# A hybrid short-convolution and HGRN2 layer: first-chunk scores of two pairs in one matmul, every second pair of four with its chunks in reverse order, one mask operation, and the second norm's column sums one product later

## The chip, the cores and the metric

The kernel runs on one core of one Trainium2 chip. The metric is the device time of one execution in microseconds (us), the median of several runs. Before the change it is 2642.1 us, from three runs of 2640.95, 2642.10 and 2642.97 us.

## The reference

One layer is applied to 2048 prompt tokens and to 64 tokens of a decoding stream with a state of its own. All arithmetic is in float32, with a model width of 1024. The part that the change touches is the HGRN2 scan: 8 heads of 128 keys and 128 values, in chunks of 64 tokens.

```
h = rms_norm(x, g_pre);  proj = h @ w_in          # ten pieces of 1024 columns
u = cA * vA;  yA = (silu(zA) * bA * causal_conv3(u)) @ w_a_out
fg = lb + (1 - lb) * sigmoid(f);  logf = log(fg);  k = 1 - fg;  q = silu(q) / sqrt(128)
for each chunk of 64 tokens, each head:            # S is the carried state
    b = cumsum(logf);  ref = b[middle]
    att = where(causal, (q * exp(b - ref)) @ (k * exp(ref - b)).T, 0)
    o = att @ v + (q * exp(b)) @ S
    S = exp(b_last) * S + (k * exp(b_last - b)).T @ v
yB = (rms_norm(o) * g_onorm * silu(zB)) @ w_b_out
out = (sigmoid(gA) * yA + sigmoid(gB) * yB) @ w_o
x = x + rms_norm(out, g_post)
x = x + (p @ w_ple_proj) * sigmoid(rms_norm(x, g_ple) @ w_ple_gate)
```

## The kernel before

**Tiling.** The 2112 tokens are worked in three blocks of 704 (`BN`). Tokens lie along the free axis and features on the 128 partitions. Big products are split into high and low parts, three matmuls of 128x352 each for one block of 128 contraction rows, and `sgroup` (lines 358 to 360) runs a seven-product scheme of the Strassen kind: each of the seven products has 4 x 3 = 12 matmuls. `in_turn` (L491 to L493) is the same scheme in another order, and `gemm` (L524 to L526, in `mm3`) is a plain product of 24 matmuls for one half of a block. The weights stream in through DMAs that SyncE issues: `raw` tiles (L194), stored low parts `lo` and `s` (L215); ScalarE casts `raw` to `hi` (L214).

**Hooks.** After each product `hook()` takes one step from a list. So small work, such as a step of attention or of a norm, stands between two products, and the engines run it while TensorE is in the next product. `spread_out` fills that list from tuples of counts: one number for each hook, saying how many steps of a generator it runs. `behind_all` and `placed` fix the order of issue: a step's instructions stand behind the last copies and additions of the products before it, and its matmuls behind the last matmul issued.

**A head.** A block of 704 tokens has 11 chunks: five pairs of two chunks (128 tokens) and one single chunk. They form three parts: four pairs, one pair, and the single chunk. For each of the 24 combinations of block and head, `head_prep` makes the operands on VectorE. `kb` holds the scaled keys of all tokens (L851), `ka` a copy of the first chunk of each pair, packed side by side (L852). In `kb` the first chunk of each pair is then scaled once more by a decay (L853), because queries of the second chunk see it from there. `qe` are the scaled queries, `vt` the values.

**Attention of a part** (`head_attn`), in four steps at four hooks. Step 1 transposes `kb` (L896) and `vt` (L898) by TensorE, 128 columns at a time, into two PSUM banks; ScalarE copies them to `kt` (L900) and `v` (L901). Then, for each pair, one float32 matmul of 64 query columns takes the first-chunk queries against `ka` (L907) and one of 64 columns takes the second-chunk queries against `kb` (L908), into a third bank `p_a` (keys on the partitions, queries along the free axis). Two predicated copies on VectorE move the entries at or below the diagonal into `att`: all columns of the upper 64 partitions (L911), and the second 64 columns of the lower 64 (L912). L911's operand `ka[:, o // 2 : o // 2 + P]` is 128 keys wide, so it holds the first chunk of the next pair too, whose scores the mask drops. The three banks of a step come from a pool of three (`pa`), so that the next part's step 1 needs each bank released. Step 2 (L918) multiplies `kt` by `v`, step 3 (L954, L956) applies `att` and the state, and step 4 (L968) transposes back.

**The norms.** `final_norm` forms the squares of eight row blocks (L633 on ScalarE), adds them up (L634 on VectorE), and then `col_rstd` sums over the partitions by small matmuls with `ones` (L615), one column each. VectorE scales the sums (L586), GpSimd takes the power (L588), and two products later `spread` (L599) brings the result back over the partitions. It does so twice, for `g_post` and for `g_ple`. In each tuple of counts, the second sum's place is one entry:

```
spread_out((norm, (0, 1, 0, 1) + (0, 1, 0) * KB + (1, 0, 1) + (0, 1) * KB))
spread_out((norms[0], (3, 0, 1, 1, 2, 2, 2, 2)), (norms[1], (0, 1, 1, 0, 1, 1, ...)))
```

The first line runs among the gate products of the next block (`sgroup`), after blocks 0 and 1. The second runs in the last block, among the plain products of the gate of block 1.

Of the kernel before, what the change touches and what calls it, by code (L numbers as in the profile page):

```python
# [12 lines left out]
I32 = mybir.dt.int32  # L13
AF = mybir.ActivationFunctionType
ALU = mybir.AluOpType
# [3 lines left out]
P = 128  # L19
D = 1024  # L20
KB = D // P
KH = KB // 2
NH = 8
CH = 64
# [58 lines left out]
def hybrid_step(  # L83
# [17 lines left out]
    V, A, G, T, SP = nc.vector, nc.scalar, nc.gpsimd, nc.tensor, nc.sync  # L101
# [3 lines left out]
    const = ctx.enter_context(tc.tile_pool(name="const", bufs=1))  # L105
# [36 lines left out]
    vec = const.tile([P, 9, KB], F32, tag="vec", name="vec")  # L142
    g_pre, g_on, g_post, g_ple = (vec[:, i, :] for i in range(4))
    cw = [vec[:, 4 + i, :] for i in range(3)]
    caus = const.tile([P, P], I32, tag="caus", name="caus")
    keep = const.tile([P, BN], F32, tag="keep", name="keep")
    atts = [
        const.tile([P, max(len(b["parts"][i]) for b in blocks), P], F32, tag=f"att{i}", name=f"att{i}") for i in range(NPART)
# [11 lines left out]
    def constants():  # L160
        tri = rt(P)
        G.memset(tri, 1.0)
        G.affine_select(
            out=tri, in_=tri, pattern=[[1, P]], compare_op=ALU.is_ge, fill=0.0, base=0, channel_multiplier=-1
        )
        V.tensor_copy(caus, tri)
        V.memset(keep, 1.0)
        V.memset(keep.rearrange("p (c t) -> p c t", t=CH)[:, :, 0:1], 0.0)
        for t in atts + lone:
            V.memset(t, 0.0)  # L170
        V.tensor_tensor(tmp, lb0, lb1, ALU.max)
        V.tensor_tensor(lb, lb0, tmp, ALU.subtract)
        V.tensor_tensor(omlb, lb1, tmp, ALU.subtract)
        A.activation(lb, lb, AF.Exp)
        A.activation(omlb, omlb, AF.Exp)
        V.tensor_tensor(tmp, lb, omlb, ALU.add)
        V.reciprocal(tmp, tmp)
        V.tensor_tensor(lb, lb, tmp, ALU.mult)
        V.tensor_scalar(omlb, lb, -1.0, 1.0, ALU.mult, ALU.add)
        V.tensor_scalar(nomlb, lb, 1.0, -1.0, ALU.mult, ALU.add)  # L180
# [624 lines left out]
    def chunks(t):  # L805
        return t.rearrange("p (c t) -> p c t", t=CH)

    def head_prep(bl, hc, hd, first, hs):
        n, npair = bl["n"], bl["npair"]
        nch, np1 = n // CH, npair * P  # L810
        sf, qe = rt(), rt()

        def sink_f(c, h, x, y):
            if c == 0:
                A.activation(half(sf, h), whole(x, y), AF.Sigmoid)
            else:
# [12 lines left out]
        qc = small.tile([P, 2, BN // CH], F32, tag="qc", name=nm("qc"))  # L829
        f, r = qc[:, 0, :nch], qc[:, 1, :nch]  # L830
        ka, kb, qx, vt, z = hf(HN + 32), rt(), rt(), rt(), rt()

        def scaled(after):


            with tc.issue_after(after):
                A.activation(r, ref.rearrange("p c o -> p (c o)"), AF.Exp)
                A.activation(eq, lg, AF.Exp)
                exps = A.activation(lg, lg, AF.Exp, scale=-1.0).ins
            with tc.issue_after(exps):  # L840
                A.activation(qe, qe, AF.Silu)
            V.tensor_tensor(f[:, 1:nch], r[:, 1:nch], chunks(eq)[:, : nch - 1, CH - 1], ALU.mult)
            V.tensor_copy(f[:, 0:1], r[:, 0:1])
            for g in bl["groups"]:
                if g["sample"]:
                    c = g["off"] // CH
                    V.tensor_copy(f[:, c : c + 1], r[:, c : c + 1])
            f1, f2 = f[:, 0 : 2 * npair : 2], f[:, 1 : 2 * npair : 2]
            ka3 = ka[:, : (nch + 1) // 2 * CH].rearrange("p (g t) -> p g t", t=CH)
            kb1 = kb[:, :np1].rearrange("p (g c t) -> p g c t", c=2, t=CH)[:, :, 0, :]  # L850
            V.tensor_tensor(kb, sf, lg, ALU.mult)  # L851
            V.tensor_copy(ka3, chunks(kb)[:, 0:nch:2, :])  # L852
            V.tensor_tensor(kb1, ka3[:, :npair, :], f2.unsqueeze(2).to_broadcast([P, npair, CH]), ALU.mult)  # L853
# [12 lines left out]

    def cols3(t, nt):
        return t[:, : nt * P].rearrange("p (g c) -> p g c", c=P)

    def head_attn(ip, gs, d, hd):  # L870
# [17 lines left out]
        def cols(t, g):  # L888
            end = g["off"] + ln
            return t[:, end - P : end]  # L890


        p_k, p_v = ps_attn(), ps_attn()
        with placed():
# [3 lines left out]
                T.transpose(p_v[:, i * P : i * P + P], cols(d["vt"], g), ident)  # L898
        kt, v = tile3(0), tile3(1)
        A.copy(kt[rows], cols3(p_k, nt)[rows])  # L900
        A.copy(v[rows], cols3(p_v, nt)[rows])  # L901
        p_a = ps_attn()
        with placed():
            for i, g in enumerate(gs):
                o = g["off"]
                if not single:
                    T.matmul(p_a[:, i * P : i * P + CH], d["ka"][:, o // 2 : o // 2 + P], qe[:, o : o + CH], start=True, stop=True)  # L907
                T.matmul(p_a[:, i * P + CH : i * P + P], cols(d["kb"], g), qe[:, o + ln - CH : o + ln], start=True, stop=True)  # L908
        pa3 = cols3(p_a, nt)
        if not single:  # L910
            V.copy_predicated(att[:CH, :nt], caus[:CH].unsqueeze(1).to_broadcast([CH, nt, P]), pa3[:CH])  # L911
        V.copy_predicated(att[CH:, :nt, CH:], caus[CH:, CH:].unsqueeze(1).to_broadcast([CH, nt, CH]), pa3[CH:, :, CH:])  # L912
        yield

        p_u = ps_attn()
# [53 lines left out]
        c = slice(o0, o0 + n)  # L969
# [374 lines left out]
    for bi, bl in enumerate(blocks):  # L1344
# [53 lines left out]
        if nxt:  # L1398
            hc = new_operands()
            ops = operands(hc, spread_all(cols), partial(load_x, nxt))  # L1400
            for j, _ in enumerate(final_out(segs, mg, xo, acc, KB - 1 if first else KH - 1)):
                if j in (1, 3, 5, 7):
                    run(ops, 1)
            fills = gates(nxt, hc, kepts[bi + 1], False)
            norm = final_norm(bl, segs, xo, acc, h2, kept, not first)
            spread_out((norm, (0, 1, 0, 1) + (0, 1, 0) * KB + (1, 0, 1) + (0, 1) * KB))
            run(fills, LEAD)
            assert not hooks
            if first:
                run(final_gate(bl, segs, h2, kept))  # L1410
        else:
            spread_out((norms[0], (3, 0, 1, 1, 2, 2, 2, 2)), (norms[1], (0, 1, 1, 0, 1, 1, 2, 2, 2, 1, 1, 2, 2, 2, 2)))
            raws = load_p(bl, G)
            for j, _ in enumerate(final_gate(blocks[bi - 1], segs, rows2, kepts[bi - 1])):
                if j == 3:
                    ph = [split_rt(raw) for raw in raws]
            run(ple(bl, ph, kept))
            assert not hooks
            first_rows = [narrow(half(t, 0)) for t in h2[:KH]]
            run(in_turn([gate_in_turn(bl, h2, xo, kept)], first_rows))  # L1420
# [49 lines left out]
```

## Time and profile before

| | |
|---|---|
| median of three runs | 2642.1 us |
| the profiled execution, its own time | 2644.82 us |
| its span, first to last instruction | 2643.1 us |
| mean granted TensorE clock | 0.995 |
| busy: TensorE, VectorE, ScalarE, GpSimd | 99%, 64%, 58%, 15% |
| HBM traffic over the span | 282 GB/s |

A page of the profile gives busy time and instructions of each engine, the chain of work that ended last, and groups of instructions by line. PE is TensorE's matmuls, PEld its weight loads, DVE VectorE, ACT ScalarE, POOL GpSimd, SP SyncE. A float32 matmul stands in the trace as two records, one for each pass. A timeline row has start, duration, engine, line, operation, output<-inputs, shape and number, and in brackets the idle time before it with what ended it.

### The profile page before, as it was taken

How to read it: one execution, taken by the hardware profiler on the slowest of the kernel's cores; microseconds unless marked ns; L12 is line 12 of the kernel's file. 1: busy time of each engine (PE TensorE's matmuls, PEld its weight loads, DVE VectorE, ACT ScalarE, POOL GpSimd, SP SyncE). 2: the span in 40 equal slices, each digit the busy share in tenths (PEclk: the TensorE clock that was granted, in tenths of full speed). 3: DMA queues.
4: the chain of work that ended last, by engine and by line, in shares of the span. 5: the costliest groups of instructions: out<-in, count | busy, mean ns of one | idle time of the engine just before them, and what ended most of it. 6: DMA issues, size and time to landing. Idle time of an engine off the chain costs nothing.

```text
span 2643.1 us, 47577 instructions
## 1 busy us (share of the span) xinstructions
PE 2609.3 (99%) x16646; PEld 2591.5 (98%) x16646; DVE 1679.8 (64%) x3229; ACT 1525.5 (58%) x2900; POOL 387.0 (15%) x713
## 2 busy tenths in 40 slices
PE   7999999999999999999999999999999999999999
PEld 7999999999999999999999999999999999999998
DVE  7688888888676555455545568553455544568756
ACT  5666665554335644567745556456667744555736
POOL 1000000210442210011112211021000101210120
PEclk9999999999999999999999999999999999999999
DMA  8678777898888997766689988599766679989977
GB/s 292 222 266 277 246 266 274 300 316 290 324 312 278 351 315 259 241 221 223 226 274 359 386 307 309 200 349 338 240 218 222 219 253 336 380 317 310 332 251 239
DMA packets 364913, 749.15 MB, mean 283 GB/s; under 512 B 44832, under 2 KB 49472, under 8 KB 364672
## 3 DMA queue, kind: packets, MB, share of 16 engines
q1 hardware_dynamic: 322560, 584.00, 64.8%
q0 software_dynamic: 41824, 162.06, 16.9%
q8 instruction: 131, 2.15, 0.3%
q14 instruction: 110, 0.90, 0.1%
q10 hardware_dynamic: 288, 0.05, 0.0%
HBM read 534.88 MB, written 211.04 MB: 282 GB/s over the span
## 4 chain that ended last, share of the span: by engine, by line
PE 90%; DMA 4%; DVE 3%; issue 2%; ACT 1%; POOL 0%; SPq 0%; ACTq 0%; DVEq 0%; POOLq 0%
PE pg L358 19%; PE pg L360 18%; PE pg L359 18%; PE pg L526 4%; PE pg L525 4%; PE pg L524 4%; PE pg L491 4%; PE pg L492 4%; PE pg L493 4%; PE pa L918 1%; PE pa L954 1%; PE pa L908 1%; PE pa L956 1%; DMA raw<-S 1%; PE pa L907 1%
## 5 line engine op out<-in xcount | busy, mean ns | idle before, releaser
L358 PE MATMUL pg<-r,hi 128*128 128x352 f32 x3304 | 1095.1, 332 | 3.4 <-DVE r L404 1.8
L359 PE MATMUL pg<-r,hi 128*128 128x352 f32 x3304 | 1068.0, 323 | 0.0
L360 PE MATMUL pg<-r,lo 128*128 128x352 f32 x2356 | 762.7, 324 | 2.1 <-DMA lo<-low 2.1
L214 ACT CAST hi<-raw 128x512 fp32r<-128x512 f32 x720 | 444.1, 619 | 524.7 <-PE pg L359 174.8
L358 PEld LDWEIGHTS pg<-r,hi 128*128 128x128 f32 x3304 | 623.1, 189 | 7.9 <-DVE r L404 3.4
L359 PEld LDWEIGHTS pg<-r,hi 128*128 128x128 f32 x3304 | 623.3, 189 | 0.0
L360 PEld LDWEIGHTS pg<-r,lo 128*128 128x128 f32 x2356 | 443.6, 188 | 2.9 <-DMA lo<-low 2.6
L360 PE MATMUL pg<-r,s 128*128 128x352 f32 x948 | 307.2, 324 | 0.0
L524 PE MATMUL pg<-r,hi 128*128 128x352 f32 x768 | 248.8, 324 | 0.5 <-ACT r L184 0.5
L525 PE MATMUL pg<-r,hi 128*128 128x352 f32 x768 | 248.9, 324 | 0.0
L184 DVE TENSOR_TENSOR r<-r,r 128x352 fp32r<-128x352 f32 (+3 forms) x298 | 183.1, 636 | 63.8 <-ACT r L184 63.1
L184 ACT CAST hi<-raw 128x512 fp32r<-128x512 f32 x218 | 134.4, 619 | 151.6 <-PE pg L359 45.1
L492 PE MATMUL pg<-r,hi 128*128 128x352 f32 x672 | 217.4, 325 | 0.0
L491 PE MATMUL pg<-r,hi 128*128 128x352 f32 x672 | 213.6, 325 | 0.1
L526 PE MATMUL pg<-r,lo 128*128 128x352 f32 x656 | 213.0, 325 | 0.0
L184 ACT CAST r<-r 128x352 fp32r<-128x352 f32 (+3 forms) x298 | 162.0, 579 | 59.2 <-DVE r L667 15.0
L184 DVE TENSOR_TENSOR lo<-raw,hi 128x512 fp32r<-128x512 f32 x218 | 149.2, 685 | 68.0 <-ACT hi L184 52.3
L360 PEld LDWEIGHTS pg<-r,s 128*128 128x128 f32 x948 | 178.9, 189 | 0.1
L184 ACT CAST hi<-s 128x512 fp32r<-128x512 f32 x160 | 98.0, 618 | 122.2 <-PE pg L359 106.4
L372 ACT COPY hf<-pg 128x352 f32<-128x352 f32 x354 | 157.1, 446 | 12.1 <-PE pg L360 11.5
L524 PEld LDWEIGHTS pg<-r,hi 128*128 128x128 f32 x768 | 144.7, 189 | 0.8 <-ACT r L184 0.8
L525 PEld LDWEIGHTS pg<-r,hi 128*128 128x128 f32 x768 | 144.8, 189 | 0.4 <-DVE r L184 0.3
(363 smaller groups left out, 4200.6 us busy)
## 6 DMA issues: line engine op xcount, KB each, us to landing
raw<-w_blk SPq DMA_DIRECT2D x570, 256.0 KB, 4.1
lo<-low SPq DMA_DIRECT2D x411, 256.0 KB, 4.2
raw<-S SPq DMA_DIRECT2D x408, 256.0 KB, 4.3
low<-lo SPq DMA_DIRECT2D x322, 256.0 KB, 3.7
s<-low SPq DMA_DIRECT2D x309, 256.0 KB, 4.3
S<-s SPq DMA_DIRECT2D x160, 256.0 KB, 3.2
r<-w_blk POOLq DMA_DIRECT2D x64, 256.0 KB, 7.0
S<-r POOLq DMA_DIRECT2D x64, 256.0 KB, 6.0
```

Of the source, the lines that this page charges most:

```text
L184: return A.copy(hi, src).ins, V.tensor_tensor(lo, src, hi.bitcast(F32), ALU.subtract).ins
L214: A.copy(hi, raw)
L358: add(hi[:, k, :], xhi, start=start and k == 0, stop=False)
L359: add(hi[:, k, :], xlo, start=False, stop=False)
L360: last[0] = add(lo[:, k, :], xhi, start=False, stop=k == KH - 1).ins
L372: copied = A.copy(got[n], ps[bank])
L491: add(hi[:, k, :], xhi, start=start and k == 0, stop=False)
L492: add(hi[:, k, :], xlo, start=False, stop=False)
L493: last[0] = add(lo[:, k, :], xhi, start=False, stop=k == KH - 1).ins
L524: T.matmul(ps, hi[:, k % 4, :], xhi[:, c], start=k == ks[0], stop=False)
L525: T.matmul(ps, hi[:, k % 4, :], xlo[:, c], start=False, stop=False)
L526: last[0] = T.matmul(ps, lo[:, k % 4, :], xhi[:, c], start=False, stop=k == ks[-1]).ins
```

## The change

Four things change; the diff below is cut to them.

1. `head_prep` builds the keys of the first four pairs so that every second pair has its two chunks in reverse order in `kb` (second chunk first). `ka` is now computed directly (L860 of the changed kernel) instead of being copied from `kb`, and `kb` is written in four pieces (L861, L862, L864, L865).
2. The first-chunk scores of two neighbouring pairs come from one matmul with 2 x 64 query columns against the 128 keys of `ka` (L929). The second pair's scores then land on the lower 64 partitions, which is why its chunks are reversed; its values in `v` are reversed too, by copies that cross from one half of the partitions to the other (L919, L920).
3. One predicated copy of 128 partitions takes the place of two of 64; its mask `caus` has a second half for the reversed pairs.
4. In three tuples of counts the second column sum moves one hook later.

```
-            kb1 = kb[:, :np1].rearrange("p (g c t) -> p g c t", c=2, t=CH)[:, :, 0, :]
-            V.tensor_tensor(kb, sf, lg, ALU.mult)
-            V.tensor_copy(ka3, chunks(kb)[:, 0:nch:2, :])
-            V.tensor_tensor(kb1, ka3[:, :npair, :], f2.unsqueeze(2).to_broadcast([P, npair, CH]), ALU.mult)
+            two = kb[:, : 4 * P].rearrange("p (c q t) -> p c q t", q=4, t=CH)
+            rest = kb[:, 4 * P : np1].rearrange("p (g c t) -> p g c t", c=2, t=CH)[:, :, 0, :]
...
+            V.tensor_tensor(ka3, chunks(sf)[:, 0:nch:2, :], chunks(lg)[:, 0:nch:2, :], ALU.mult)
+            V.tensor_tensor(two[:, :, 1:3, :], pairs(sf, 1), pairs(lg, 1), ALU.mult)
+            V.tensor_tensor(kb[:, 4 * P :], sf[:, 4 * P :], lg[:, 4 * P :], ALU.mult)
+            by = f2[:, :4].rearrange("p (c e) -> p c e", e=2).unsqueeze(3).to_broadcast([P, 2, 2, CH])
+            V.tensor_tensor(two[:, :, 0:4:3, :], ka3[:, :4, :].rearrange("p (c e) t -> p c e t", e=2), by, ALU.mult)
+            V.tensor_tensor(rest, ka3[:, 4:npair, :], f2[:, 4:npair].unsqueeze(2).to_broadcast([P, npair - 4, CH]), ALU.mult)
...
-        A.copy(v[rows], cols3(p_v, nt)[rows])
+        pv3 = cols3(p_v, nt)
+        if nt == 4:
+            A.copy(v[:, 0:4:2, :], pv3[:, 0:4:2, :])
+            A.copy(v[:CH, 1:4:2, :], pv3[CH:, 1:4:2, :])
+            A.copy(v[CH:, 1:4:2, :], pv3[:CH, 1:4:2, :])
+        else:
+            A.copy(v[rows], pv3[rows])
...
-                if not single:
-                    T.matmul(p_a[:, i * P : i * P + CH], d["ka"][:, o // 2 : o // 2 + P], qe[:, o : o + CH], start=True, stop=True)
+                if not single and i % 2 == 0:
+                    m = min(2, nt - i)
+                    T.matmul(firsts(p_a, i * P, m), d["ka"][:, o // 2 : o // 2 + P], firsts(qe, o, m), start=True, stop=True)
...
-        if not single:
-            V.copy_predicated(att[:CH, :nt], caus[:CH].unsqueeze(1).to_broadcast([CH, nt, P]), pa3[:CH])
-        V.copy_predicated(att[CH:, :nt, CH:], caus[CH:, CH:].unsqueeze(1).to_broadcast([CH, nt, CH]), pa3[CH:, :, CH:])
+        if single:
+            V.copy_predicated(att[CH:, :1, CH:], caus[CH:, :1, CH:], pa3[CH:, :, CH:])
+        elif nt == 1:
+            V.copy_predicated(att, caus[:, :1], pa3)
+        else:
+            att4, pa4 = (x.rearrange("p (c e) t -> p c e t", e=2) for x in (att[:, :nt], pa3))
+            V.copy_predicated(att4, caus.unsqueeze(1).to_broadcast([P, nt // 2, 2, P]), pa4)
...
-            spread_out((norm, (0, 1, 0, 1) + (0, 1, 0) * KB + (1, 0, 1) + (0, 1) * KB))
+            spread_out((norm, (0, 1, 0, 1) + (0, 1, 0) * KB + (0, 1, 0, 1) + (0, 1) * KB))
...
-            spread_out((norms[0], (3, 0, 1, 1, 2, 2, 2, 2)), (norms[1], (0, 1, 1, 0, 1, 1, 2, 2, 2, 1, 1, 2, 2, 2, 2)))
+            spread_out((norms[0], (3, 0, 0, 1, 1, 2, 2, 2, 2)), (norms[1], (0, 1, 1, 0, 1, 1, 2, 2, 2, 1, 1, 2, 2, 2, 2)))
```

The set-up of `caus` gains two small casts and two fills on VectorE. Line numbers of the changed kernel are higher: L896, L898, L908 and L918 are L911, L913, L930 and L944 there, L615 is L619, L358 to L360 are L362 to L364.

TensorE, four pairs of one head of block 0: transposes of `kb` and `vt`, then the scores into bank `pa`. Before:

```order
L896 MATMUL pa_1885<-ident,r_1410 128x128 x4
L898 MATMUL pa_1886<-ident,r_1412 128x128 x4
L907 MATMUL pa_1899<-r_1150,hf_1409 128x64
L908 MATMUL pa_1899<-r_1150,r_1410 128x64
L907 MATMUL pa_1899<-r_1150,hf_1409 128x64
L908 MATMUL pa_1899<-r_1150,r_1410 128x64
L907 MATMUL pa_1899<-r_1150,hf_1409 128x64
L908 MATMUL pa_1899<-r_1150,r_1410 128x64
L907 MATMUL pa_1899<-r_1150,hf_1409 128x64
L908 MATMUL pa_1899<-r_1150,r_1410 128x64
```

The same place of the changed kernel, on TensorE (`hf` is `ka`, the second `r` of L930 is `kb`):

```order
L911 MATMUL pa_1891<-ident,r_1414 128x128 x4
L913 MATMUL pa_1892<-ident,r_1416 128x128 x4
L929 MATMUL pa_1907<-r_1156,hf_1413 128x2x64
L930 MATMUL pa_1907<-r_1156,r_1414 128x64 x2
L929 MATMUL pa_1907<-r_1156,hf_1413 128x2x64
L930 MATMUL pa_1907<-r_1156,r_1414 128x64 x2
```

Eight score matmuls became six. The one pair of the next part keeps its two matmuls, the single chunk its one.

TensorE, the second column sums among the gate products that follow block 0; `pg` is the product's bank, `s` or `lo` its weights' low part. Before:

```order
L358 MATMUL pg_11616<-r_10860,hi_11576 128x352
L359 MATMUL pg_11616<-r_10860,hi_11576 128x352
L360 MATMUL pg_11616<-r_10860,s_11577 128x352
L615 MATMUL pa_11631<-ones,r_10987 128x1 x3
L615 MATMUL pa_11638<-ones,r_10987 128x1 x3
L358 MATMUL pg_11645<-r_10362,hi_11582 128x352
L359 MATMUL pg_11645<-r_10363,hi_11582 128x352
L360 MATMUL pg_11645<-r_10362,lo_11583 128x352
```

The same place of the changed kernel, on TensorE (bank `pg_11635` is the product that was `pg_11645` before):

```order
L362 MATMUL pg_11635<-r_10873,hi_11586 128x352
L363 MATMUL pg_11635<-r_10874,hi_11586 128x352
L364 MATMUL pg_11635<-r_10873,lo_11587 128x352
L619 MATMUL pa_11650<-ones,r_10991 128x1 x3
L619 MATMUL pa_11657<-ones,r_10991 128x1 x3
L362 MATMUL pg_11664<-r_10366,hi_11592 128x352
L363 MATMUL pg_11664<-r_10367,hi_11592 128x352
L364 MATMUL pg_11664<-r_10366,s_11593 128x352
```

The sums moved behind the next product of 12 matmuls. The spreading back (L599, L603 after) stays two products behind the sums.

ScalarE, the copies of the four pairs' `kt` and `v` and what stands behind them. Before:

```order
L372 COPY hf_1883<-pg_1870 128x352
L900 COPY r_1895<-pa_1885 128x512
L901 COPY r_1896<-pa_1886 128x512
L184 CAST hi_1854<-raw_1808 128x512
L372 COPY hf_1923<-pg_1910 128x352
```

The same place of the changed kernel, on ScalarE:

```order
L376 COPY hf_1889<-pg_1876 128x352
L915 COPY r_1901<-pa_1891 128x512
L918 COPY r_1902<-pa_1892 128x2x128
L919 COPY r_1902<-pa_1892 64x2x128
L920 COPY r_1902<-pa_1892 64x2x128
L188 CAST hi_1860<-raw_1814 128x512
L376 COPY hf_1928<-pg_1915 128x352
```

One copy became three, and the cast and the copy behind it stand behind all three.

More of the change, by code (lines that the diff above doesn't have):

```diff
@@ L144, in hybrid_step @@
     cw = [vec[:, 4 + i, :] for i in range(3)]
-    caus = const.tile([P, P], I32, tag="caus", name="caus")
+    caus = const.tile([P, 2, P], I32, tag="caus", name="caus")
     keep = const.tile([P, BN], F32, tag="keep", name="keep")
@@ L165, in constants @@
         )
-        V.tensor_copy(caus, tri)
+        V.tensor_copy(caus[:, 0, :], tri)
+        V.memset(caus[:, 1, :], 0)
+        V.tensor_copy(caus[:CH, 1, CH:], tri[:CH, :CH])
+        V.tensor_copy(caus[CH:, 1, :CH], tri[CH:, CH:])
+        V.memset(caus[CH:, 1, CH:], 1)
         V.memset(keep, 1.0)
@@ L849, in scaled, with pairs @@
             ka3 = ka[:, : (nch + 1) // 2 * CH].rearrange("p (g t) -> p g t", t=CH)
-            kb1 = kb[:, :np1].rearrange("p (g c t) -> p g c t", c=2, t=CH)[:, :, 0, :]
-            V.tensor_tensor(kb, sf, lg, ALU.mult)
-            V.tensor_copy(ka3, chunks(kb)[:, 0:nch:2, :])
-            V.tensor_tensor(kb1, ka3[:, :npair, :], f2.unsqueeze(2).to_broadcast([P, npair, CH]), ALU.mult)
+            two = kb[:, : 4 * P].rearrange("p (c q t) -> p c q t", q=4, t=CH)
+            rest = kb[:, 4 * P : np1].rearrange("p (g c t) -> p g c t", c=2, t=CH)[:, :, 0, :]
+            def pairs(x, at):
+                return x[:, : 4 * P].rearrange("p (c e h t) -> p c e h t", e=2, h=2, t=CH)[:, :, :, at, :]
+            V.tensor_tensor(ka3, chunks(sf)[:, 0:nch:2, :], chunks(lg)[:, 0:nch:2, :], ALU.mult)
[4 more added lines that the diff above has]
+            V.tensor_tensor(rest, ka3[:, 4:npair, :], f2[:, 4:npair].unsqueeze(2).to_broadcast([P, npair - 4, CH]), ALU.mult)
             V.tensor_tensor(f2, f2, f1, ALU.mult)
@@ L890, in cols, with firsts @@
             return t[:, end - P : end]
+        def firsts(t, o, n):
+            return t[:, o : o + n * P].rearrange("p (g c t) -> p g c t", c=2, t=CH)[:, :, 0, :]
         p_k, p_v = ps_attn(), ps_attn()
```

## The prediction

> **What bounds the kernel now.** I read the page first: busy time of each engine and the chain that ended last.
>
> ```profile
> PE 2609.3 (99%) x16646; PEld 2591.5 (98%) x16646; DVE 1679.8 (64%) x3229; ACT 1525.5 (58%) x2900; POOL 387.0 (15%) x713
> PE 90%; DMA 4%; DVE 3%; issue 2%; ACT 1%; POOL 0%; SPq 0%; ACTq 0%; DVEq 0%; POOLq 0%
> ```
>
> TensorE is busy 2609.3 of 2643.1 us and holds 90% of the chain. So there are two ways to gain: less work on TensorE, or fewer of its 34 us of idle time. The list of what TensorE waited for says which idle time is within reach of this change.
>
> ```profile
> PE pa L615 <- DVE r L634: 5.8, 3, 2.0
> PE pg L360 <- DMA lo<-low: 2.1, 2, 1.9
> ...
> PE pa L898 <- DVE r L404: 1.2, 1, 1.2
> ```
>
> The column sums (L615) waited 5.8 us in three waits, and the change moves exactly these. No score, transpose or state matmul (L896, L907, L908, L918) stands in that list with more than 1.2 us (one L898 in the first head), so attention is paid for in TensorE's own time, not in waits. DMA has cost TensorE only 2.1 us.
>
> **Part 1: fewer score matmuls.** The first-chunk matmuls, by line, then four pairs of one head and, for comparison, matmuls of twice the columns in the timeline:
>
> ```profile
> L907 PE MATMUL pa<-r,hf x240: 221/275/294, 105.3 to 2115.2; 128*128 128x64 f32 x120
> ```
> ```profile
> 1211.57 0.39 PE L908 MATMUL pa<-r,r 128*128 128x64 f32 x2
> ...
> 1212.91 0.39 PE L908 MATMUL pa<-r,r 128*128 128x64 f32 x2
> ```
> ```profile
> 120.41 0.39 PE L956 MATMUL pa<-r,r 128*128 128x128 f32 x2
> ...
> 121.30 0.39 PE L956 MATMUL pa<-r,r 128*128 128x128 f32 x2
> ```
>
> The 240 records are 120 matmuls of two passes: 24 heads (three blocks of eight) by five pairs. After the change a head has three (two for four pairs, one for the fifth pair), so 24 x 2 = 48 go. Between the two rows of 1211.57 and 1212.91 lie six matmuls of 64 columns: (1212.91 - 1211.57) / 6 = 0.223 us each. Between 120.41 and 121.30 lie four of 128 columns: 0.89 / 4 = 0.223 us each. Twice the columns cost the same here, so a merged matmul costs what one of its halves did, and 48 x 0.223 = 10.7 us go. No row shows a float32 matmul whose columns come in two pieces of 64. The bounds are 0.223 us (contiguous 128 columns) and 2 x 0.223 us (it runs as its two halves; then this part gains nothing). I take the first, since the 128-column rows have the same count of columns and the same weights.
>
> A page speaks against it. The Trainium skill, "TensorE: Matmul & The Clock Gate", section "Back-to-back issue gap", has about 60 cycles for 1 to 64 columns and 134 for 128, so that two halves cost as much as the whole; by that the part gains about nothing. The equal 0.223 us above disagree for this kernel's stream, in which each matmul loads new weights; the same page's section "LDWEIGHTS (loading the stationary operand)" has a load time that goes by the 128 weight columns alone, which would explain it.
>
> **Part 2: the column sums.** The three places in the timeline:
>
> ```profile
> 915.55 0.32 PE L358 MATMUL pg<-r,hi 128*128 128x352 f32 x1
> ...
> 917.34 0.32 PE L360 MATMUL pg<-r,s 128*128 128x352 f32 x1
> ...
> 919.66 1.47 PE L615 MATMUL pa<-ones,r 128*128 128x1 f32 x12 [2.00 <-DVE r L634]
> ```
> ```profile
> 1773.17 0.32 PE L360 MATMUL pg<-r,lo 128*128 128x352 f32 x1
> 1775.49 2.32 PE L615 MATMUL pa<-ones,r 128*128 128x1 f32 x12 [2.00 <-DVE r L634]
> ```
> ```profile
> 2540.36 0.32 PE L524 MATMUL pg<-r,hi 128*128 128x352 f32 x1
> 2542.47 0.80 PE L615 MATMUL pa<-ones,r 128*128 128x1 f32 x6 [1.78 <-DVE r L634]
> ```
>
> A product's 12 matmuls start from 915.55 to 917.34, so one takes 1.79 / 11 = 0.163 us and a product 1.95 us. Counted from when the next matmul could have started (0.16 us after the last), the sums lost 2.16, 2.16 and 1.95 us. They waited for the last addition on VectorE, which hangs on squares on ScalarE and on earlier steps, not on the product that now slips in. So that product runs inside the wait: 1.95 us are won at each of the first two places, with 0.2 us of waiting left, and all 1.95 us at the third, where the next product is a plain one of 24 matmuls (3.9 us). Sum 5.9 us. What is late next: the spreading back stays two products behind at the first two places, and no wait for it stands in the list of before. The norm's later steps keep their own time while TensorE runs about 2 us ahead of them; GpSimd's DMA issues for the spills (L1169) follow those steps and come no earlier.
>
> **Part 3: the clock behind the waits.** Stretches of 2 us with the granted clock (third column from the right), at the first place, the third last and the wait for a DMA at 1061:
>
> ```profile
> 920.00:922.00 2.00, 2.00 (x17) 2.00 (x17) 0.32 (x2) 0.35 (x2) 1.58 (x3) 1.00 1.06 394
> 1774.00:1776.00 2.00, 0.51 (x5) 0.54 (x5) 1.31 (x2) 2.00 (x5) 0.92 (x2) 0.98 1.03 396
> 1776.00:1778.00 2.00, 2.00 (x10) 2.00 (x11) 0.31 (x2) 0.18 (x1) 1.04 (x2) 0.50 1.08 401
> 1778.00:1780.00 2.00, 2.00 (x8) 2.00 (x8) 0.01 (x1) 0.00 (x0) 0.85 (x1) 0.50 1.03 397
> 1780.00:1782.00 2.00, 2.00 (x9) 2.00 (x8) 0.00 (x0) 0.67 (x2) 0.00 (x0) 0.50 0.89 343
> 1782.00:1784.00 2.00, 2.00 (x12) 1.97 (x11) 0.00 (x0) 0.32 (x2) 0.00 (x0) 0.82 0.83 270
> 2542.00:2544.00 2.00, 1.53 (x11) 1.56 (x12) 1.02 (x3) 0.47 (x2) 0.45 (x1) 0.98 0.86 313
> 2544.00:2546.00 2.00, 2.00 (x9) 2.00 (x8) 1.17 (x2) 0.00 (x0) 1.24 (x2) 0.50 0.26 95
> 2546.00:2548.00 2.00, 2.00 (x12) 1.93 (x10) 0.45 (x1) 0.00 (x0) 2.00 (x5) 0.67 0.48 180
> 1062.00:1064.00 2.00, 2.00 (x10) 2.00 (x10) 0.17 (x1) 0.42 (x1) 0.00 (x0) 0.63 1.05 403
> ```
>
> Behind two of the three waits at L615 the clock falls to 0.50 for a while, and it falls behind the 1.9 us wait for a DMA too; behind the wait at 919 it stays at 1.00. Lost time is 2 us times the missing share: 0.04 + 1.00 + 1.00 + 1.00 + 0.36 = 3.4 us at 1775, and 0.04 + 1.00 + 0.66 = 1.7 us at 2543. With waits of 0.2 us in their place I take both as gone: 5.1 us. The bounds are nothing (the falls come for another reason) and these 5.1 us.
>
> The same page's "Part 1: The HAM clock gate" puts the clock to half after an idle window of about 3.4 us that runs freely. By the letter of it a 2 us wait is too short to trip the gate, and the 5.1 us would stay; the rows show the fall behind waits of 1.8 to 2.0 us, not always, which fits a free-running window with a lower bar.
>
> **Part 4: VectorE and ScalarE, beside TensorE.** Groups by shape, and where a head's copies and the next bank's use stand:
>
> ```profile
> L851 DVE TENSOR_TENSOR r<-r,r 128x704 f32<-128x704 f32 x24 | 21.3, 887 | 2.5 <-ACT r L839 1.9
> L853 DVE TENSOR_TENSOR r<-hf,qc 128x320 f32<-128x320 f32 x24 | 11.7, 489 | 0.6
> L852 DVE COPY hf<-r 128x384 f32<-128x384 f32 x24 | 8.4, 351 | 0.0
> L912 DVE COPY_PREDICATED att<-caus,pa 64x256 f32<-64x256 int32 x24 | 10.8, 451 | 0.3
> L901 ACT COPY r<-pa 128x512 f32<-128x512 f32 x24 | 14.3, 597 | 2.8 <-PE pa L898 2.8
> L901 ACT COPY one<-pa 128x128 f32<-128x128 f32 x24 | 6.7, 279 | 0.0
> ```
> ```profile
> 1212.09 0.60 ACT L901 COPY r<-pa 128x512 f32<-128x512 f32 x1
> 1215.20 0.62 ACT L214 CAST hi<-raw 128x512 fp32r<-128x512 f32 x1 [2.51 <-issue]
> ```
> ```profile
> 1215.23 0.27 PE L898 MATMUL pa<-ident,r 128*128 128x128 f32 x1
> ```
>
> VectorE's operands: 887 + 489 + 351 = 1727 ns go. From 704 and 320 elements, one costs 1.036 ns and an instruction 157 ns; 384, 256, 192, 256 and 64 elements come to 555 + 422 + 356 + 422 + 223 = 1978 ns. That is 0.25 us more a head, while the second mask operation (0.45 us and two shorter ones) goes: about 0.4 us less a head, on an engine at 64%. I count it at nothing. ScalarE's `v` copy of 0.60 us becomes three of 256 elements, 385 ns each between the 128- and 512-element rows, so 1.16 us: 0.56 us more a head. Its cover: the copy ends at 1212.69, and the bank it frees is written next by L898 at 1215.23, 2.5 us later. Behind the copies stands a cast that starts at 1215.20, after 2.51 us in which ScalarE did nothing. If the cover were gone, it would cost up to 0.56 x 24 = 13 us. Bounds for a copy of 64 partitions are 279 and 597 ns; at the upper one it is 1.2 us more, still covered. The mask's set-up adds under 1 us, once, on VectorE.
>
> **The sum.** 10.7 + 5.9 + 5.1 = 21.7 us. The profiled execution took 2644.82 us, which gives 2623.1; it lies 2.7 us above the median of the runs, which gives 2620.4. That difference is larger than a short fall of the clock (1.7 us), so the runs may have one less to win back. I set 2621.5.
>
> **Rivals.** (a) The falls of the clock are not the waits' doing, or come back at other places: 5.1 us less, 2626.6. For it: the wait at 919 had none. Against: the other two and the one at 1061 did. (b) The merged matmul runs as its halves: 10.7 us less, 2632.2. Against: the equal 0.223 us. (c) A DMA takes the place of the sums' wait. For it: the rows at 1774 to 1782 have DMA shares of 0.89 to 1.08 at 343 to 401 GB/s, so weights could be short once TensorE gives no time back. Against: right after that wait the cast of the next weights was itself waiting for TensorE, not for data:
>
> ```profile
> 1781.33 0.62 ACT L214 CAST hi<-raw 128x512 fp32r<-128x512 f32 x1 [5.14 <-PE pg L359]
> ```
>
> All of parts 2 and 3 would go: 2631.4. (d) The change does not do what it says: the sums wait as long behind the next product, because the last addition slips by the same product; the time is that of (c). (e) Slower: the three copies hold the transposes' bank. That needs them to end past the 2.5 us of cover in every head; each us beyond costs 24 us. It is slower than before from 0.9 us beyond (21.7 / 24), and at 1.2 us beyond gives 2620.4 + 28.8 = 2649. The 2.51 us of idle ScalarE behind the copies speak against it.
>
> **How the numbers follow.** Forecast 0.68, with its own range of 2617 to 2625 (the wait of 1.9 us for a DMA at 1061 and the fall of the clock behind it may go or double); (a) 0.12; (b) 0.06; (c) and (d) 0.08; (e) 0.06. The range of 80% reaches from 2616.5 to (b): 2632.5. A measurement of this kernel tells about 0.2% from no change, 5.3 us. (a) to (d) alone are faster by more, and so are 0.90 in all; of (b), (c) and (d) I count 0.04 as failing together, which leaves nothing to gain and is the same; (e) is slower, 0.06.
>
> **What would show it.** Right: 72 x 2 records at L929 with starts 0.22 us apart, scores of four pairs 0.45 us shorter; L619 with waits under 0.3 us; no half clock at the two places. Wrong: records at L929 twice as far apart; TensorE waiting at L619 or for `lo` or `hi` behind it; L913 waiting for ScalarE's L920.

## The result and the profile after

The changed kernel takes 2634.29 us (median of six runs, 2628.84 to 2636.60); six runs of the kernel before beside it have a median of 2642.55 us. The ratio is 0.9963, with a 95% interval of 0.9953 to 0.9974: about 8 us are won, where 21.7 were forecast. The profiled execution after took 2636.60 us, with a span of 2634.9 us and a granted clock of 0.995, the same as before.

Busy time of the engines and the chain that ended last, from the page after:

```profile
PE 2600.3 (99%) x16550; PEld 2582.7 (98%) x16550; DVE 1666.3 (63%) x3233; ACT 1538.5 (58%) x2948; POOL 386.9 (15%) x713
...
PE 92%; DMA 3%; DVE 2%; issue 1%; ACT 1%; POOL 0%; SPq 0%; ACTq 0%; DVEq 0%; POOLq 0%
```

TensorE has 96 records fewer (48 matmuls of two passes) and 9.0 us less of busy time. ScalarE has 13.0 us more, VectorE 13.5 us less. TensorE's idle time has hardly changed: 2643.1 - 2609.3 = 33.8 us before, 2634.9 - 2600.3 = 34.6 us now. So the matmuls went, and the waits did not, though DMA now holds 3% of the chain and VectorE 2%, one point less each. What TensorE waited for, in total, times and longest (us):

```profile
PE pa L619 <- DVE r L638: 5.2, 2, 4.8
...
PE pg L364 <- DMA lo<-low: 2.2, 2, 2.0
...
PE pa L913 <- DVE r L408: 1.4, 1, 1.4
```

The column sums wait 5.2 us in two places, against 5.8 us in three before. One of them is 4.8 us, more than twice the longest before. The three places in the timeline of the kernel after:

```profile
917.76 1.47 PE L619 MATMUL pa<-ones,r 128*128 128x1 f32 x12
...
1768.54 1.47 PE L619 MATMUL pa<-ones,r 128*128 128x1 f32 x12 [0.47 <-DVE r L638]
...
2532.16 1.27 PE L619 MATMUL pa<-ones,r 128*128 128x1 f32 x6 [4.75 <-DVE r L638]
```

The wait of 2.00 us at the first place is gone, that at the second is 0.47 us, and that at the third has grown from 1.78 to 4.75 us. The granted clock there (third column from the right):

```profile
918.00:920.00 2.00, 2.00 (x18) 2.00 (x18) 0.32 (x2) 1.43 (x4) 1.59 (x3) 1.00 1.05 389
...
1770.00:1772.00 2.00, 2.00 (x12) 2.00 (x12) 0.16 (x1) 0.63 (x2) 1.33 (x2) 0.78 1.04 399
1772.00:1774.00 2.00, 2.00 (x9) 2.00 (x8) 0.53 (x1) 0.97 (x2) 0.00 (x0) 0.50 1.02 400
...
2532.00:2534.00 2.00, 1.84 (x8) 1.87 (x9) 0.54 (x3) 0.07 (x1) 0.28 (x1) 0.58 0.85 320
2534.00:2536.00 2.00, 2.00 (x8) 2.00 (x8) 1.33 (x2) 0.00 (x0) 1.25 (x2) 0.50 0.01 5
2536.00:2538.00 2.00, 2.00 (x8) 2.00 (x8) 0.00 (x0) 0.00 (x0) 2.00 (x4) 0.50 0.47 180
2538.00:2540.00 2.00, 2.00 (x12) 1.93 (x11) 0.66 (x2) 0.46 (x1) 0.67 (x2) 0.72 0.81 256
```

At the second place the half clock lasts half as long as before (3.4 us by the clock's own records, 6.8 before); at the third twice as long (6.8 us against 3.4).

**Where the time went, product by product.** Both traces hold the same 14,712 product matmuls (128x352) in the same order, so each can be set against its twin. The start of the twin moves earlier by 2.0 us at the first place and 2.6 us at the second, and comes back by 4.6 us at the third. Over the heads of the second and third blocks it moves earlier by 0.45 us a head.

**Which sum the third wait belongs to.** The last tuple moves the second sum of `norms[0]`. In the timeline of before that sum stands here:

```profile
2514.48 0.72 PE L615 MATMUL pa<-ones,r 128*128 128x1 f32 x6
```

It has no bracket: it never waited. The sum at 2542.47 that waited 1.78 us is the second sum of `norms[1]`, whose tuple the change leaves alone. The prediction took the one for the other.

Counted in the two traces, the moved sum doesn't even come later on TensorE: 13,992 product matmuls stand before it in both (it starts at 2501.89 after). What the later entry moves are the steps around that sum: its spreading, which had 14,004 product matmuls before it and now has 14,016, and steps of both norms on VectorE and GpSimd.

**What that sum waits for.** The chain of work in a window says it better than the list of waits, which names only the last addition. First the kernel before, cut to its two ends (start, duration, what):

```profile
2521.61 5.33 DMA r<-x_fm
...
2527.04 0.13 DVE r L1160
...
2541.80 0.54 DVE r L634
2542.33 0.14 issue
2542.47 0.80 PE pa L615 x6
```

Then the kernel after:

```profile
2519.24 0.54 POOL y_fm L1221
2519.78 5.35 DMA r<-x_fm
2525.33 0.27 issue
2525.59 0.89 DVE r L1219
2526.48 0.80 DVE r L188
2527.28 0.80 DVE r L1220
2528.08 0.81 DVE r L188
2528.89 0.99 DVE r L1199 x2
2529.88 0.45 DVE r L1186
2530.35 0.51 ACT r L637
2530.86 0.53 DVE r L638
2531.49 0.54 DVE r L638
2532.16 1.27 PE pa L619 x6
...
2534.23 0.29 PE pg L528
...
2538.33 0.29 PE pg L530
```

Both chains come from a load of `x_fm`, the layer's input that the norm adds (L1186, L1160 before). GpSimd issues it (L1176) behind a write of `y_fm` (L1221), whose data VectorE forms first (L1220). Before, it is the load of an earlier step. After the change it is the last but one: when VectorE gets it at 2525.15, it still has 3.3 us of other work (L1219, L188, L1220, L188) and two steps of `norms[0]` (L1199) queued in front of the last additions. Before, the same four instructions stood ahead of the addition of that load, from 2535.66 to 2538.87, and covered its landing. (The last two rows are for the price of a half clock, further down.) VectorE's waits for `x_fm` between 2480 and 2545 us, in total, times and longest, before and after:

```profile
DVE r L1160 <- DMA r<-x_fm: 2.0, 1, 2.0
```
```profile
DVE r L1186 <- DMA r<-x_fm: 5.2, 2, 2.8
```

VectorE waits 3.2 us more for the load, and TensorE 3.0 us more for the sum. That is the theory which the experiments test. Its rivals were: the two steps of `norms[0]` that slipped in between are to blame, or TensorE simply comes earlier by what the scores save.

### The profile page after: what moved, and what is told of

Same layout as the page of the kernel before. It is cut to its first block, busy times and chain, and to the rows that moved or that the text cites. A ratio compares the mean times of both kernels' runs of the same rounds, so it can differ in the third digit from the quotient of the medians.

```text
span 2634.9 us, 47400 instructions
## 1 busy us (share of the span) xinstructions
PE 2600.3 (99%) x16550; PEld 2582.7 (98%) x16550; DVE 1666.3 (63%) x3233; ACT 1538.5 (58%) x2948; POOL 386.9 (15%) x713
## 4 chain that ended last, share of the span: by engine, by line
PE 92%; DMA 3%; DVE 2%; issue 1%; ACT 1%; POOL 0%; SPq 0%; ACTq 0%; DVEq 0%; POOLq 0%
PE pg L362 19%; PE pg L364 19%; PE pg L363 19%; PE pg L529 5%; PE pg L530 5%; PE pg L528 5%; PE pg L495 4%; PE pg L496 4%; PE pg L497 4%; PE pa L980 1%; PE pa L944 1%; PE pa L982 1%; PE pa L930 1%; DMA raw<-S 1%; DMA r<-x_fm 1%
## 5 line engine op out<-in xcount | busy, mean ns | idle before, releaser
L362 PE MATMUL pg<-r,hi 128*128 128x352 f32 x3304 | 1094.8, 331 | 4.2 <-DVE r L408 2.6
L364 PE MATMUL pg<-r,lo 128*128 128x352 f32 x2356 | 763.2, 324 | 2.2 <-DMA lo<-low 2.2
L362 PEld LDWEIGHTS pg<-r,hi 128*128 128x128 f32 x3304 | 623.0, 189 | 9.0 <-DVE r L408 4.0
L364 PEld LDWEIGHTS pg<-r,lo 128*128 128x128 f32 x2356 | 443.6, 188 | 2.9 <-DMA lo<-low 2.8
L364 PE MATMUL pg<-r,s 128*128 128x352 f32 x948 | 307.2, 324 | 0.0
L188 ACT CAST hi<-raw 128x512 fp32r<-128x512 f32 x218 | 134.3, 620 | 152.9 <-PE pg L363 46.1
L188 DVE TENSOR_TENSOR r<-r,r 128x352 fp32r<-128x352 f32 (+3 forms) x298 | 183.1, 636 | 63.8 <-ACT r L188 62.9
L188 ACT CAST r<-r 128x352 fp32r<-128x352 f32 (+3 forms) x298 | 161.9, 578 | 61.9 <-DVE r L671 17.4
L188 DVE TENSOR_TENSOR lo<-raw,hi 128x512 fp32r<-128x512 f32 x218 | 149.3, 686 | 68.1 <-ACT hi L188 59.3
L364 PEld LDWEIGHTS pg<-r,s 128*128 128x128 f32 x948 | 178.6, 188 | 0.0
L188 ACT CAST hi<-s 128x512 fp32r<-128x512 f32 x160 | 98.1, 619 | 123.8 <-PE pg L363 112.8
L376 ACT COPY hf<-pg 128x352 f32<-128x352 f32 x354 | 157.0, 446 | 12.2 <-PE pg L364 11.6
```

Of the source, the lines that this page charges most:

```text
L188: return A.copy(hi, src).ins, V.tensor_tensor(lo, src, hi.bitcast(F32), ALU.subtract).ins
L362: add(hi[:, k, :], xhi, start=start and k == 0, stop=False)
L364: last[0] = add(lo[:, k, :], xhi, start=False, stop=k == KH - 1).ins
L376: copied = A.copy(got[n], ps[bank])
```

## The experiments

Each kernel was timed over several rounds beside the kernel before on the same chip, whose medians were 2642.75 us in the first group of four, 2643.36 us in the second and 2642.86 us in the third group of three.

### The two halves of the change

The scores alone, with the tuples as before (two are changed; the first of them runs after block 0 and again after block 1, which makes the three places):

```
-            spread_out((norm, (0, 1, 0, 1) + (0, 1, 0) * KB + (0, 1, 0, 1) + (0, 1) * KB))
+            spread_out((norm, (0, 1, 0, 1) + (0, 1, 0) * KB + (1, 0, 1) + (0, 1) * KB))
...
-            spread_out((norms[0], (3, 0, 0, 1, 1, 2, 2, 2, 2)), (norms[1], (0, 1, 1, 0, 1, 1, 2, 2, 2, 1, 1, 2, 2, 2, 2)))
+            spread_out((norms[0], (3, 0, 1, 1, 2, 2, 2, 2)), (norms[1], (0, 1, 1, 0, 1, 1, 2, 2, 2, 1, 1, 2, 2, 2, 2)))
```

> The change without its three moved column sums: all tuples of counts as before, the heads as in the change. Theory: the merged score matmuls give what product starts in the two traces show, 0.38 to 0.45 us a head, 24 heads, 10.1 us: about 2632.5 us against 2642.5, and the three waits at the column sums stay at 2.0, 2.0 and 1.8 us, within 0.3. Rival (TensorE being some 10 us ahead makes the last column sum's wait longer, not the moved entry): that wait grows to 4 us or more, and the time is about 2636.

Measured: 2632.04 us (2630.94 to 2635.16), ratio 0.9959 [0.9945, 0.9972]. That is 10.7 us less than before, with an interval from 7.4 to 14.5 us, and 2 us less than the whole change, which the intervals don't tell apart. The sums wait three times, 6.1 us in all, with 2.58 us at the second place, more than expected, and 1.71 us at the last; so TensorE's earlier arrival does not make the last wait longer, and that rival falls.

The sums alone, the kernel before with the changed tuples (the same lines with + and - exchanged):

> The kernel before with the three moved column sums and nothing else. Theory: the waits after blocks 0 and 1 fall to under 0.6 us, which is worth 3.4 us and up to 3.4 us of clock; the last tuple moves a sum that did not wait and makes the other one wait some 3 us longer, so the whole is about nothing, 2638 to 2643 us. Rival (the prediction's reading, that the third wait is at a moved sum): 2631.5 us.

Measured: 2639.04 us (2635.60 to 2642.72), ratio 0.9987 [0.9978, 0.9996]. The first two waits are gone, the last one is 3.92 us. So the long wait comes from the tuples and not from the scores, and the tuples together win 3.7 us where 11.0 were forecast.

### The last tuple

The change with the last tuple as before:

```
-            spread_out((norms[0], (3, 0, 0, 1, 1, 2, 2, 2, 2)), ...)
+            spread_out((norms[0], (3, 0, 1, 1, 2, 2, 2, 2)), ...)
```

> The change with the last tuple of counts as before; the other two sums stay moved. Theory: the last wait at a column sum falls from 4.8 us to about 1.8 us, worth 3.0 us and up to 3.4 us of clock: 2628 to 2631.5 us against 2634.3 of the change. Rival (the wait grew because TensorE is ahead): the wait stays at 4 to 5 us, and the time at 2634.

Measured: 2626.44 us (2624.09 to 2629.10), ratio 0.9939 [0.9926, 0.9951]. Taking one zero out of one tuple wins 7.9 us over the change, more than the theory's 2.8 to 6.3 us (2628 to 2631.5 us), and the last wait is 1.15 us. Against the scores alone, the first tuple wins 5.6 us.

The same, with the sum that did wait, that of `norms[1]`, one product later:

```
-... (norms[1], (0, 1, 1, 0, 1, 1, 2, 2, 2, 1, 1, 2, 2, 2, 2))
+... (norms[1], (0, 1, 1, 0, 1, 1, 2, 2, 2, 0, 1, 1, 2, 2, 2, 2))
```

> As with the last tuple put back, and the column sum that really waits there (the second half's second one) moved one plain product later. Theory: its wait is gone (under 0.3 us) and with it the fall of the clock behind it, so 1.8 us and 1.7 to 3.4 us better than with the last tuple put back alone: 2625 to 2628 us. Rival (the norm's last additions slip with it): the wait stays near 2 us or more, and the time is that of the kernel with the last tuple put back.

Measured: 2623.97 us (2622.91 to 2627.69), ratio 0.9931 [0.9919, 0.9944]; no sum waits over 0.1 us any more. This is faster than both kernels and 1 us below the theory's range; against the last tuple put back it is 2.5 us less, where the intervals overlap.

The change with both sums later (the tuple of `norms[0]` as changed, that of `norms[1]` with the zero):

> The change with one more entry moved: the second column sum of norms[1] comes one product later too. Theory (what counts at the last place is only when TensorE asks for the sum of norms[1]; a product of 3.9 us before it covers the wait of 4.75 us almost): no wait over 1 us at L619 in the last place, at most one fall of the clock there, about 6 to 8 us less than the change, 2626 to 2628 us. Rival (VectorE's order slips by the same product, since the steps of norms[0] stand ahead in any case): the wait stays at 3 us or more and the time at 2632 to 2635 us.

Measured: 2626.74 us (2625.73 to 2628.38), ratio 0.9934 [0.9922, 0.9947]. The sum still waits 1.68 us at the last place, with no fall of the clock behind it, where VectorE waits 4.8 us for `x_fm`; so the product in between covers about 3 us of the lateness. The time is the theory's, the wait is between it (under 1 us) and the rival (3 us or more).

### The load

The change with four loads of `x_fm` asked for ahead in the last block, and not two:

```
-        for _ in range(2 if bl["last"] else 4):
+        for _ in range(4 if bl["last"] else 4):
```

> The change with four instead of two loads of x_fm asked for ahead in the last block's norms, so that the last two stand on GpSimd's queue before the write of y_fm. Theory (VectorE stood 2.4 us waiting for x_fm with 3.4 us of other work queued behind, and that made the last sum late): the wait at L1186 is gone and the wait at L619 falls from 4.75 us by 2 to 3 us, the time by 2 to 5 us to 2629 to 2632 us. Rival (it is only the two steps of norms[0] that now stand in between, 1.2 us of VectorE): the wait at L619 stays over 4 us and the time at 2634 us.

Measured: 2624.00 us (2622.95 to 2625.80), ratio 0.9924 [0.9910, 0.9938], 9.8 us less than the change in the same group, about twice the most that the theory expected, and faster than both kernels, level with the sum of `norms[1]` moved. The queue of GpSimd and the sum, from two windows of the timeline:

```profile
2506.17 1.09 POOL L1176 DMA_DIRECT2D r<-x_fm  x2
2510.78 0.55 POOL L1221 DMA_DIRECT2D y_fm<-r  x1 [3.53 <-issue]
...
2521.18 0.76 PE L619 MATMUL pa<-ones,r 128*128 128x1 f32 x6
```

The last two loads now stand ahead of the write that held them up, no wait for `x_fm` is left on VectorE, and the sum starts without a wait. The expectation was too small because it left the first of VectorE's two waits out and the falls of the clock too: set against the change product by product, 8.1 us are won at this place, where the change had a wait of 4.75 us and 6.8 us at half clock. The rival, the two steps of `norms[0]`, falls: they stand where they stood in the change.

The kernel before with the loads ahead (the same edit), and nothing of the change:

> The kernel before, with four instead of two loads of x_fm asked for ahead in the last block's norms, and nothing of the change. Theory (the load was behind the third wait of before too: VectorE stood 2.0 us at L1160 for x_fm): the third wait at L615 shrinks from 1.78 us to under 0.3 us and the clock does not fall behind it, 1.8 + 1.7 = 3.5 us less, about 2639.5 us; the first two waits stay at 2.0 us. Rival (the load only costs where the entry of norms[0] was moved): no change, 2642 to 2643 us.

Measured: 2641.63 us (2639.68 to 2643.40), ratio 0.9994 [0.9986, 1.0003]. In the trace the third wait and the fall behind it are gone, and the matmul behind that place has moved earlier by 3.4 us against its twin, as the theory had it (3.5). By the clock of the whole it is 1.2 us less and not told apart from nothing: in this trace the clock fell for 6.8 us behind each of the first two waits, where before had one such fall. The load is behind the third wait of before too; that the total gains by it is not shown.

The loads ahead with the entry of `norms[0]` put back:

> The change with the loads of x_fm ahead and the entry of norms[0] as before: merged scores, the sums of the first two places one product later. Theory (the moved entry did harm only by queueing VectorE behind a load that had not landed; with the loads early it is neutral): the same as with the loads ahead alone, 2624 us within 1.5 us. Rival (the moved entry costs by itself, by the two steps it pushes between): 2 us or more faster, 2622 us or less.

Measured: 2626.07 us (2623.03 to 2626.91), ratio 0.9935 [0.9922, 0.9947]; the loads ahead alone gave 0.9924 [0.9910, 0.9938] in another group. That is 2.1 us more than with the loads ahead alone, where the theory allowed 1.5; the intervals overlap, and at the last place the products of the two traces keep within 0.2 us of each other. So no cost of the moved entry by itself is seen once the loads are early, and the rival, which had this kernel 2 us or more faster, falls.

The wait of the sum follows that of the load in every trace. Both in us, VectorE's for `x_fm` and TensorE's at the last sum, which stands within six matmuls of its old place in all of these:

| kernel | VectorE for `x_fm` | TensorE at the sum | half clock there |
|---|---|---|---|
| before | 2.0 | 1.78 | 3.4 |
| the scores alone | 1.9 | 1.71 | 3.4 |
| the sums alone | 4.4 | 3.92 | 6.8 |
| the last tuple back | 1.5 | 1.15 | 3.4 |
| the merge undone (below) | 4.8 | 4.54 | 6.8 |
| the change | 5.2 | 4.75 | 6.8 |
| the change again (below) | 6.0 | 5.59 | 6.8 |
| the loads ahead, in four kernels | 0 | 0 | 0 |

### The merge

The change with the merge undone; layout, copies, mask and tuples stay:

```
-                if not single and i % 2 == 0:
-                    m = min(2, nt - i)
-                    T.matmul(firsts(p_a, i * P, m), d["ka"][:, o // 2 : o // 2 + P], firsts(qe, o, m), start=True, stop=True)
+                if not single:
+                    k0 = o // 2 - CH * (i % 2)
+                    T.matmul(p_a[:, i * P : i * P + CH], d["ka"][:, k0 : k0 + P], qe[:, o : o + CH], start=True, stop=True)
```

> The change, with its key layout, copies, mask and the three tuples, but each of the four pairs has a first-chunk matmul of its own again (64 columns): 48 matmuls are back. Theory (a score matmul costs 0.223 us for 64 and for 2 x 64 columns alike): 48 x 0.223 = 10.7 us more than the change, about 2645 us. Rival (the merged matmul runs as its two halves, and the gain came from the key layout or the single mask operation): the same as the change, about 2634 us.

Measured: 2639.97 us (2638.06 to 2646.33), ratio 0.9988 [0.9979, 0.9997]; 6.2 us more than the change in the same group, short of 10.7, so the rival falls. This was inconclusive about the size, so it was tried again where no long wait stands at the end.

The merge undone, with the loads ahead (both edits above):

> The change with the loads of x_fm ahead and the merge undone: 48 first-chunk matmuls of 64 columns are back. Undoing the merge in the change itself cost 6 us by the medians where 10.7 were expected. Theory (48 x 0.223 us all count, and what was missing was hidden in the long last wait and in falls of the clock that come or not): with that wait gone, 10.7 us more than the loads ahead alone, 2634.7 us. Rival (part of each matmul is hidden beside other work): 6 us more, 2630 us.

Measured: 2636.26 us (2630.20 to 2637.07), ratio 0.9968 [0.9955, 0.9980], against 0.9924 for the loads ahead: 12.3 us by the medians of two groups, and 10.2 us more than the kernel above, with the entry of `norms[0]` put back too, in the same group. The traces settle the size: set against that kernel, the products of this one fall back by 0.45 us at the four pairs of a head 24 times, 10.7 us in all. The rest of the differences is waits and falls of the clock that come in one execution and not in another.

The changed kernel again, unedited:

> The changed kernel itself, unedited, on the same chip as the others of this group. 2634 us, a wait of 4 to 5 us at L619 in the last place with two falls of the clock there (6.8 us at half); at the first two places the wait is under 0.6 us. If a fall of the clock needs a wait above some length, no fall stands behind the waits under 0.4 us; if it is the single-column matmuls alone, a fall stands there in some executions whatever the wait.

Measured: 2633.80 us (2630.01 to 2634.43), ratio 0.9957 [0.9944, 0.9970]. The last sum waited 5.59 us in this execution with 6.8 us of half clock behind it, and at the first two places stood no wait over 0.1 us and no fall.

## Why the prediction was right or wrong

**Part 1 was right, in mechanism and size.** It predicted 10.7 us, and the scores alone win 10.7 us. That the medians agree to a tenth is luck; the size rests on the traces, below and in the last undoing of the merge. (The operand `ka` of 128 keys is that of the matmul L907, not of the mask operation L911, as is said ahead of the prediction.) The four pairs of the head of the prediction, after the change:

```profile
1205.95 0.39 PE L929 MATMUL pa<-r,hf 128*128 128x128 f32 x2
1206.17 0.56 PE L930 MATMUL pa<-r,r 128*128 128x64 f32 x4
1206.57 0.44 PE L929 MATMUL pa<-r,hf 128*128 128x128 f32 x2
1206.84 0.56 PE L930 MATMUL pa<-r,r 128*128 128x64 f32 x4
1207.21 0.41 PE L362 MATMUL pg<-r,hi 128*128 128x352 f32 x1
```

The same place before, its first row and the one behind its last score:

```profile
1211.40 0.33 PE L907 MATMUL pa<-r,hf 128*128 128x64 f32 x2
...
1213.11 0.41 PE L358 MATMUL pg<-r,hi 128*128 128x352 f32 x1
```

From the first score to the next product it is 1207.21 - 1205.95 = 1.26 us for six matmuls, where eight took 1213.11 - 1211.40 = 1.71 us: 0.45 us less. So a matmul whose columns come in two pieces of 64 costs what one piece costs, 0.21 to 0.22 us, and rival (b) falls. The Trainium skill, "TensorE: Matmul & The Clock Gate", section "Back-to-back issue gap", has a table of isolated matmuls that would have made this gain nothing; the runs speak against applying it to these matmuls, each with new weights.

**Part 2 was right at two places and wrong at the third, and that is the failed step.** At the first two the wait fell from 2.00 us to none and 0.47 us, about as forecast (0.2). At the third the prediction said that the moved sum waits 1.95 us too long and that "the sums" all hang on ScalarE and earlier steps. The wait there belonged to a sum that the change doesn't move, and it hung on a load; the sum that the change does move stands behind the same products as before, so no product came to run inside a wait. Moving the entry of `norms[0]` changed the order on VectorE and GpSimd ahead of that sum, so that the load's landing was no longer covered, and the wait grew by 3.0 us. A term of +1.95 us (and 1.7 us of clock) became a loss. The list of waits named the last releaser only; the chain of work in the window 2523 to 2545 of before, with 5.33 us of `x_fm` at its start, would have named the load. Rival (c) said that a DMA takes the place of the sums' wait. A DMA did, but another one: not the weights at the first two places, where no such wait over 0.2 us came, but `x_fm` at the third.

**Part 3 was right in kind, and too neat.** In the ten traces with the first tuple moved the clock fell once at the first two places: for 3.4 us, behind the 0.47 us of the change's first profile. So rival (a) was right there in a small way. At the third place the fall doubled with the wait. The price of a fall was a little high: in the chain of after, 14 product matmuls lie between 2534.23 and 2538.33, 0.293 us each and not 0.163, so 3.4 us of half clock cost 3.4 x (1 - 0.163 / 0.293) = 1.5 us, where the prediction had 1.7.

**Part 4 was right.** Busy time and mean duration of the copies and of the operations on VectorE, from the groups by shape:

```profile
L938 DVE COPY_PREDICATED att<-caus,pa 128x512 f32<-128x512 int32 x24 | 18.0, 749 | 50.5 <-PE pa L930 50.5
...
L918 ACT COPY r<-pa 128x256 f32<-128x256 f32 x24 | 9.2, 384 | 2.8 <-PE pa L913 2.8
L919 ACT COPY r<-pa 64x256 f32<-64x256 f32 x24 | 8.9, 370 | 0.3
L920 ACT COPY r<-pa 64x256 f32<-64x256 f32 x24 | 8.8, 365 | 0.3
```

The three copies take 384 + 370 + 365 = 1119 ns (1155 forecast), those across the halves no more than the plain one, and ScalarE's 13.0 us more are what was forecast (24 x 0.56 = 13.4). None of it reaches TensorE: its one wait at L913, which is for VectorE, is 1.4 us, 1.2 before. Rival (e) falls, and with the waits at the first two places gone so does (d).

**The sum again.** By medians: 10.7 us for the scores, 5.6 us for the first tuple (forecast 2 x 1.95 + 3.4 = 7.3), and 7.9 us lost at the last tuple (forecast 3.65 won). That makes 8.4 us, against 8.3 us measured. Of the 13.4 us that the forecast was off, 11.6 are the third place. Of the 7.9 us lost there, the trace shows 5.1 when its products are set against those of the kernel with the last tuple back. The other 2 to 3 us stay open. The runs of one kernel differ by as much at the start, where one wait (L433) was 4.3 us in the first profile of the change and 1.5 in the second.

The rivals' times are counted from two bases, (a) and (b) from the 2621.5 us that were set, (c) to (e) from 2620.4; from 2621.5 the time of (c) is 2632.5 and not 2631.4. The upper end of the range, 2632.5, is likewise 0.3 us above the time of (b) that it names. Neither changes a chance.

## What to carry to other kernels

Before a wait is moved, find out which instance of the line it is, and follow its chain back past the last releaser: the list of waits said "the addition", the chain of the window said "a load, 20 us earlier". A step that is put one hook later also moves its place in every in-order queue, and what it lets slip in front of a load's first use can cost more than the wait that it was to fill. A load that is asked for one step earlier is the cheaper cure: here it made the order of the sums in the last block harmless, without a wait to place.

## What the runs showed of the hardware

**The half clock keeps to a grid.** In the traces the clock's changes lie whole multiples of 3.413 us apart; in that of before, the falls at 1062.52, 1775.91 and 2543.91 us are 209 and 225 such steps apart. After the start a fall lasts one or two steps. Counting in each step the time without a matmul of more than one column, in all thirteen traces from 85 us on: each of the 29 full-clock steps with 1.87 us or more of it (16 before 2600 us, the others at the program's end) was followed by a half-clock step, of three with 1.81 to 1.83 us two were, and below 1.75 us only one was (1.38 us, with the loads ahead and the merge undone). So a wait of 0.47 us falls too if the 1.3 us of one-column matmuls behind it lie in the same step, and a wait of 2.00 us goes free if a step's border cuts it, as at 919 before. The Trainium skill, "TensorE: Matmul & The Clock Gate", "Part 1: The HAM clock gate", has a free-running window of 3413 ns, and the traces agree; it puts the fall behind an idle window, and here a step that was little over half idle was enough.

**One-column matmuls count as idle for that clock**, by the same count: the twelve of a sum are on TensorE's row as busy, at 917.76 for 1.47 us. Were they counted as work, the step before the fall at 1771.13 of the changed kernel would hold 0.47 us without a matmul and three more steps before a fall 0.79 to 1.15 us, while steps with 1.64 to 1.74 us stand in other traces without a fall.
